# A hybrid diffusion step on one core: triangular blocks turned by VectorE, condition vectors on four column groups, six stores moved

## Chip, core and metric

One core of one Trainium2 chip. The time is device microseconds of one execution of the whole program; lower is better. Times are the median of the runs shown.

## What is computed

One layer of a backbone on 128 prompt tokens and 2048 latent tokens of width 1024, then a final RMSNorm. A layer is:

```python
mod = silu(cond) @ ada_w + ada_b            # shift, scale, gate: 3 x 1024
h = rmsnorm(x, norm_g) * (1 + scale) + shift
p = h @ w_in                                # 1024 -> 2832 columns
y_a = gated DeltaNet, two directions, 4 heads of 64, chunks of 64 tokens
y_b = spatial gating MLP; y_c = pooling minus identity; y_d = 2-D DFT, real part
out = concat(y_a, y_b, y_c, y_d) @ w_out
x + gate * out
```

DeltaNet needs, for each chunk, head and direction, the inverse of a 64x64 unit triangular matrix (`Tinv` in the reference), and a scan over chunks that carries a 64x64 state. Everything is float32; the kernel also returns the prompt's last scan states.

## The kernel before

The kernel is written in a tile framework: each operation is bound to an engine by hand, and a planner at build time puts the operations in an order for each engine by priority (program order, moved by offsets), by when their inputs are ready in its model, and by free buffers. So an edit can change the order of operations that it does not name. All transfers are issued from the queue of SP, in order.

The tokens are 17 tiles of 128, in three groups (12, 12 and 10 chunks of 64).

**Prologue.** `ada_load` brings a quarter of the shift and scale weights, 4 tiles of 512 KB, and `mod_q` (L377) multiplies them by the two condition vectors: of each quarter two tiles as float32 (L386; a float32 matmul is two passes, two instructions in the trace) and two split into a rounded part and a rest by ScalarE or VectorE (L391 to L394) and multiplied as float32r (L397). The result lies as 4 rows of 512 columns; L403 turns it into columns. Meanwhile `x_prep` loads x tiles, adds the position table and scales by the norm; `x_fin` (L334) transposes them on TensorE (L342), ScalarE applies scale and shift (L344), VectorE and GpSimd split the result into `hT`. The list `late` holds six x tiles; L467 stores them to `xs_d`, from which the output phase reads them again.

**Projections.** `mm3` (L250) is three float32r products for one float32 product; its matmuls are most of TensorE's work. `proj_cm` calls `tick` after each piece, and `tick` advances the generators in the list `work`: `lanes` of a group, later `gate_rows`. One step is taken if one generator is in the list, two if there are more.

**The triangular inverse.** `pair_pre` (L647) builds, for a pair of heads, products of keys in PSUM (L673, L703) with decays; the two 32x32 diagonal blocks of each 64x64 matrix go to `Ld`, the block between them to `Lo`. A lane is one diagonal block; `lanes_in` (L727) puts a lane on a partition with 32 transposes on TensorE (L731) for each group and 16 ScalarE copies (L734). `lanes_solve` (L736) runs 30 steps of two VectorE operations each (L741, L743) on all lanes. `lanes_out` (L750) goes back: 128 small products with the identity for each group (L767, two instructions each), after 4 strided VectorE copies (L762), then copies with masks on ScalarE (L771), on VectorE (L772) and to `XE` on ScalarE (L775). Two chains of 32x32 products (L783 to L793) fill in the block between. `rec_out` stores the results for the scan.

**After phase A.** `gate_rows` (L1283) multiplies the last third of `ada_w` by the condition vectors, float32 with two columns of weights (L1295), out of two of the four buffers of the pool `xp_`; the remaining branches, the scan (L1033 on), the Fourier branch and the output projection (`out_tile`) follow.

PSUM has tags of `pj` 3, `pa` 2, `pb` 2 and `pc` 1 banks. `x_fin` in phase A uses `pc` alone, key products use `pb`, the lanes use `pa`.

Of the kernel before, what the change touches and what calls it, by code (L numbers as in the profile page):

```python
# [9 lines left out]
F32 = mybir.dt.float32  # L10
# [7 lines left out]
D = 1024  # L18
# [126 lines left out]
def tile_dit_step(ctx: ExitStack, tc: tile.TileContext, io: dict, dbg=None, stop=None):  # L145
# [112 lines left out]
    c4 = cst.tile([128, KC, 4], F32R, name="c4")  # L258
    nc.scalar.activation(c4[:, :, 0:2], csil, AF.Copy)
    nc.vector.tensor_tensor(c4[:, :, 2:4], csil, c4[:, :, 0:2].bitcast(F32), op=ALU.subtract)  # L260
    s42 = cst.tile([4, 2], F32, name="s42")
    nc.vector.tensor_tensor(s42, ident[0:4, 0:2], ident[0:4, 2:4], op=ALU.add)
# [71 lines left out]
    def x_fin(prep, fs=range(KC), pss=(pc,)):  # L334
        with hp(OXv[0]):
# [3 lines left out]
            for f in fs:  # L339
# [7 lines left out]
                if spill is not None:  # L347
                    nc.sync.dma_start(out=h_d[spill, :, f, off:off + 384], in_=h[:, :384])

# [12 lines left out]
    with tc.tile_pool(name="ada", bufs=3, reuse_waits="tile") as ada_p:  # L362
        OXv[:] = [0, 0]
        c40 = ada_p.tile([128, KC, 4], F32, name="c40", bufs=1)
        nc.vector.memset(c40, 0.0)
        nc.vector.tensor_copy(c40[:, :, 0:2], csil)
# [10 lines left out]
        def mod_q(q, ts):  # L377
            ps = pb()
            for s in range(2):
                for k0 in range(0, KC, 4):  # L380
                    t = ts[2 * s + k0 // 4]
                    sp = ("0", "0", "1", "2")[2 * s + k0 // 4]
                    o = ps[0:4, s * 256:s * 256 + 256]
                    if sp == "0":
                        for k in range(4):
                            nc.tensor.matmul(o, c40[:, k0 + k], t[:, k], start=(k0 + k == 0), stop=(k0 + k == KC - 1))  # L386
                        continue
                    hi = ada_p.tile([128, 4, 256], F32R, tag="adh", name="adh", bufs=2)
                    lo = ada_p.tile([128, 4, 256], F32R, tag="adl", name="adl", bufs=2)
                    if sp == "1":  # L390
                        nc.scalar.activation(hi, t, AF.Copy)  # L391
                    else:
                        nc.vector.tensor_copy(hi, t)
                    nc.vector.tensor_tensor(lo, t, hi.bitcast(F32), op=ALU.subtract)  # L394
                    for e, w in enumerate((hi, lo)):
                        for k in range(4):
                            nc.tensor.matmul(o, c4[:, k0 + k], w[:, k],  # L397
                                             start=(k0 + k + e == 0), stop=(k0 + k + e == KC))
# [1047 lines left out]
```

## Time and profile before

| | us |
|---|---|
| median of 3 runs | 1212.36 (1209.45 to 1213.25) |
| the profiled execution, its own time | 1211.1 |
| its span, first to last instruction | 1209.3 |
| TensorE busy / VectorE busy / ScalarE busy | 1090.1 / 815.1 / 417.9 |

The profiled execution stands 1.26 us under the median. Its granted TensorE clock is 0.952 of full on the mean. In the trace PE is TensorE's matmuls, PEld its weight loads, DVE is VectorE, ACT ScalarE, POOL GpSimd, SPq the queue of SP.

### The profile page before, as it was taken

How to read it: one execution, taken by the hardware profiler on the slowest of the kernel's cores; microseconds unless marked ns; L12 is line 12 of the kernel's file. 1: busy time of each engine (PE TensorE's matmuls, PEld its weight loads, DVE VectorE, ACT ScalarE, POOL GpSimd, SP SyncE). 2: the span in 40 equal slices, each digit the busy share in tenths (PEclk: the TensorE clock that was granted, in tenths of full speed). 3: DMA queues.
4: the chain of work that ended last, by engine and by line, in shares of the span. 5: the costliest groups of instructions: out<-in, count | busy, mean ns of one | idle time of the engine just before them, and what ended most of it. 6: DMA issues, size and time to landing. Idle time of an engine off the chain costs nothing.

```text
span 1209.3 us, 29864 instructions
## 1 busy us (share of the span) xinstructions
PE 1090.1 (90%) x12211; PEld 986.3 (82%) x12211; DVE 815.1 (67%) x1864; ACT 417.9 (35%) x837; POOL 432.6 (36%) x429
## 2 busy tenths in 40 slices
PE   5888988998799698898979989898999889999997
PEld 2488977998779697875879888887899778999997
DVE  3666886799974699934884633784243488878665
ACT  2355667656565756123123111121111211111211
POOL 1347364726442237510231242232135343433212
PEclk9899998999879799898999999999999989999999
DMA  9879549943644564645264556589355645544331
GB/s 309 302 250 316 139 120 232 279 131 83 148 114 104 126 151 112 192 142 143 70 187 125 160 165 211 181 262 306 89 160 167 213 136 166 173 133 150 106 131 70
DMA packets 251391, 204.28 MB, mean 169 GB/s; under 512 B 109138, under 2 KB 218706, under 8 KB 250998
## 3 DMA queue, kind: packets, MB, share of 16 engines
q1 hardware_dynamic: 251254, 202.37, 56.7%
q8 instruction: 96, 1.57, 0.5%
q14 instruction: 41, 0.34, 0.1%
HBM read 138.86 MB, written 63.46 MB: 167 GB/s over the span
## 4 chain that ended last, share of the span: by engine, by line
PE 45%; DVE 17%; DMA 11%; issue 4%; ACT 3%; SPq 1%; POOL 1%; DVEq 0%; ACTq 0%; POOLq 0%
PE pj L250 34%; PE pa L1053 3%; DMA wst<-in_wt_dram 2%; DVE LL L743 2%; DVE ltmp L741 2%; DVE BIG L243 2%; DVE acc L842 1%; DMA X<-xd_d 1%; DMA ada<-in_ada_dram 1%; PE pb L1295 1%; DMA hr<-h_d 1%; DMA wos<-in_wo_dram 1%; DVE BIG L240 1%; DMA wst<-in_wv_dram 1%; PE pb L1393 1%
## 5 line engine op out<-in xcount | busy, mean ns | idle before, releaser
L250 PE MATMUL pj<-BIG 128*128 128x256 f32 (+4 forms) x3888 | 615.9, 313 | 16.7 <-ACT g L1222 4.0
L250 PEld LDWEIGHTS pj<-BIG 128*128 128x128 f32 x3888 | 560.9, 195 | 36.2 <-issue 10.8
L250 PE MATMUL pj<-BIG,yh 128*128 128x256 f32 x1088 | 197.5, 286 | 3.6 <-ACT BIG L1355 2.4
L243 POOL TENSOR_TENSOR BIG<-wst,BIG 128x512 fp32r<-128x512 f32 (+1 forms) x66 | 96.0, 1455 | 235.4 <-DVE BIG L240 137.3
L250 PEld LDWEIGHTS pj<-BIG,yh 128*128 128x128 f32 x1088 | 164.6, 190 | 7.0 <-ACT BIG L1355 2.6
L250 PE MATMUL pj<-BIG,yl 128*128 128x256 f32 x544 | 141.3, 284 | 0.0
L250 PEld LDWEIGHTS pj<-BIG,yl 128*128 128x128 f32 x544 | 98.7, 190 | 0.7
L240 DVE CAST BIG<-wst 128x512 fp32r<-128x512 f32 (+2 forms) x72 | 38.6, 540 | 74.8 <-DMA wst<-in_wt_dram 34.5
L1060 POOL TENSOR_TENSOR gS<-S,sc_s 128x256 f32<-128x256 f32 x32 | 20.9, 655 | 133.8 <-DVE S L1075 128.3
L842 DVE SCALAR_TENSOR_TENSOR acc<-raw,prm,acc 128x768 f32<-128x768 f32 (+1 forms) x72 | 64.2, 908 | 5.5 <-ACT acc L840 5.5
L1374 ACT ACTIVATE yh<-yt 128x768 fp32r<-128x768 f32 (+1 forms) x34 | 20.7, 629 | 128.9 <-issue 47.3
L1222 ACT ACTIVATE g<-pj 128x256 f32<-128x256 f32 (+1 forms) x64 | 23.3, 396 | 118.3 <-PE pj L250 111.8
L243 DVE TENSOR_TENSOR BIG<-wst,BIG 128x512 fp32r<-128x512 f32 (+1 forms) x66 | 53.4, 808 | 15.9 <-ACT BIG L242 13.8
L1413 POOL TENSOR_TENSOR z<-z,xs 128x1024 f32<-128x1024 f32 x16 | 41.8, 2612 | 57.1 <-DVE z L1405 52.0
L741 DVE TENSOR_TENSOR ltmp<-LL 128x60 f32<-128x60 f32 (+14 forms) x90 | 53.6, 595 | 4.5 <-ACT LL L734 3.1
L743 DVE TENSOR_TENSOR LL<-LL,ltmp 128x60 f32<-128x60 f32 (+14 forms) x90 | 55.3, 614 | 1.4
L242 ACT ACTIVATE BIG<-wst 128x512 fp32r<-128x512 f32 (+1 forms) x60 | 37.6, 632 | 35.3 <-DMA wst<-in_wt_dram 14.0
L354 POOL TENSOR_TENSOR BIG<-h,BIG 128x384 fp32r<-128x384 f32 (+2 forms) x28 | 26.7, 953 | 54.0 <-DVE BIG L353 37.4
L1075 DVE TENSOR_TENSOR S<-pa,gS 128x256 f32<-128x256 f32 x34 | 14.3, 420 | 42.1 <-PE pc L1053 35.0
L1375 DVE TENSOR_TENSOR yl<-yt,yh 128x768 fp32r<-128x768 f32 (+1 forms) x34 | 37.3, 1112 | 7.8 <-ACT yh L1374 7.8
L1405 DVE TENSOR_TENSOR z<-pj,gbc 128x256 f32<-128x256 f32 x68 | 26.0, 419 | 22.5 <-PE pj L250 22.2
L1071 ACT ACTIVATE xn<-pa 128x256 f32<-128x256 f32 x34 | 12.9, 381 | 80.8 <-PE pa L1053 73.2
(291 smaller groups left out, 1846.1 us busy)
## 6 DMA issues: line engine op xcount, KB each, us to landing
wst<-in_wt_dram SPq DMA_DIRECT2D x96, 256.0 KB, 3.5
R<-rec_d SPq DMA_DIRECT2D x136, 128.0 KB, 3.1
ada<-in_ada_dram SPq DMA_DIRECT2D x24, 512.0 KB, 5.3
C<-com_d SPq DMA_DIRECT2D x68, 128.0 KB, 3.1
xs<-xs_d SPq DMA_DIRECT2D x16, 512.0 KB
out_dram<-z SPq DMA_DIRECT2D x16, 512.0 KB, 3.1
x<-in_xs_dram SPq DMA_DIRECT2D x13, 512.0 KB
xs_d<-x SPq DMA_DIRECT2D x13, 512.0 KB, 6.1
```

The source lines that it names most:

```text
L240: nc.vector.tensor_copy(hi[:, ks, a:a + w], st[:, :, :w])
L242: nc.scalar.activation(hi[:, ks, a:a + w], st[:, :, :w], AF.Copy)
L243: (nc.vector if k0 == 0 else nc.gpsimd).tensor_tensor(lo[:, ks, a:a + w], st[:, :, :w], hi[:, ks, a:a + w].bitcast(F32), op=ALU.subtract)
L250: nc.tensor.matmul(out, lh[a](k), rh[b](k), start=(k == first and i == 0), stop=(k == last and i == 2))
L354: (nc.gpsimd if f % 2 else nc.vector).tensor_tensor(hT[1][:, f, off:off + w], h, hi.bitcast(F32), op=ALU.subtract)
L741: nc.vector.tensor_tensor(tv, X[:, :, j, j + 1:32].unsqueeze(2).to_broadcast([128, 2, j, ni]), bc(X[:, :, 0:j, j], ni), op=ALU.mult)
L743: nc.vector.tensor_tensor(X[:, :, 0:j, j + 1:32], X[:, :, 0:j, j + 1:32], tv, op=ALU.add)
L842: nc.vector.scalar_tensor_tensor(o, raw[:, si + j:si + j + n], w[:, j:j + 1], o, op0=ALU.mult, op1=ALU.add)
L1053: nc.tensor.matmul(ps[o, q], lh(q)[hp], rh[hp, q])
L1375: nc.vector.tensor_tensor(yl[:, q], yt[:, q], yh[:, q].bitcast(F32), op=ALU.subtract)
L1405: nc.vector.tensor_tensor(z[:, ns], ps, gbc[:, cd, ns], op=ALU.mult)
L1413: nc.gpsimd.tensor_tensor(z, z, xs, op=ALU.add)
```

## The change

It has five parts. (1) The lanes are formed and undone by VectorE transposes of 32x32 blocks: two in `lanes_in` and four in `lanes_out` for each group, each over 1024 elements of 128 partitions; the sign moves into the factor `nb`; ScalarE copies diagonal blocks into `XA`, whose other halves GpSimd clears; `LL` has one buffer. (2) The products of keys take PSUM from `pa`, and `x_fin` in phase A alternates between `pc` and `pa`. (3) `mod_q` and `gate_rows` multiply by 32 columns of weights (two of them not zero) at one of four column positions, all in float32 and without a split; a product with `gsum` adds the four parts. (4) A store of 6x8 elements from `h67` to `xs_d` stands ahead of the six stores of `late`, which write over it and so come after it. (5) Steps of the generators: `lanes` has 20 where it had 30, `gate_rows` 10 where it had 16.

```diff
-    c4 = cst.tile([128, KC, 4], F32R, name="c4")
...
+    c32 = cst.tile([128, KC, 32], F32, name="c32")
+    nc.gpsimd.memset(c32, 0.0)
+    nc.vector.tensor_copy(c32[:, :, 0:2], csil)
+
+    def strip_mm(ps, k, w):
+        g = 32 * (k % 4)
+        nc.tensor.matmul(ps[g:g + 32], c32[:, k], w, start=k < 4, stop=k >= 4, tile_position=(0, g))
+
+    gsum = cst.tile([128, 2], F32, name="gsum")
+    nc.vector.tensor_tensor(gsum, ident[:, 0:2], ident[:, 32:34], op=ALU.add)
+    for j in (64, 96):
+        nc.vector.tensor_tensor(gsum, gsum, ident[:, j:j + 2], op=ALU.add)
@@ mod_q @@
-                for k0 in range(0, KC, 4):
-                    t = ts[2 * s + k0 // 4]
-                    sp = ("0", "0", "1", "2")[2 * s + k0 // 4]
...
-                    nc.vector.tensor_tensor(lo, t, hi.bitcast(F32), op=ALU.subtract)
-                    for e, w in enumerate((hi, lo)):
-                        for k in range(4):
-                            nc.tensor.matmul(o, c4[:, k0 + k], w[:, k],
-                                             start=(k0 + k + e == 0), stop=(k0 + k + e == KC))
-            rows = ada_p.tile([4, 512], F32, tag="mrow", name="mrow", bufs=1)
-            nc.scalar.activation(rows, ps[0:4, :], AF.Copy)
+                for k in range(KC):
+                    strip_mm(ps[:, s * 256:s * 256 + 256], k, ts[2 * s + k // 4][:, k % 4])
+            rows = ada_p.tile([128, 512], F32, tag="mrow", name="mrow", bufs=1)
+            nc.scalar.activation(rows, ps, AF.Copy)
             ps = pb()
             for j in range(4):
-                nc.tensor.matmul(ps[:, 2 * j:2 * j + 2], rows[:, j * 128:(j + 1) * 128], s42)
+                nc.tensor.matmul(ps[:, 2 * j:2 * j + 2], rows[:, j * 128:(j + 1) * 128], gsum)
@@ prologue @@
-        x_fin(p1, (6, 7), (pa,))
+        h67 = x_fin(p1, (6, 7), (pa,))
         xd_k(range(3), 3)
         x_fin(p2, range(8), (pc, pa))
         fold_pool()
+        nc.sync.dma_start(out=xs_d[0:len(late), 0, 0:8], in_=h67[0:len(late), 0:8])
         for i, xt in late:
             nc.sync.dma_start(out=xs_d[i], in_=xt)
@@ scalars @@
+        nc.vector.tensor_scalar(g.nb, g.be, -1.0, None, op0=ALU.mult)
@@ pair_pre (both products: keys by keys, keys by queries) @@
-            ps = pb()
+            ps = pa()
...
-            nc.gpsimd.tensor_tensor(Ldv[:, pair, d], Ldv[:, pair, d], bc(g.be[:, pair, d], 32), op=ALU.mult)
+            nc.gpsimd.tensor_tensor(Ldv[:, d], Ldv[:, d], bc(g.nb[:, pair, d], 32), op=ALU.mult)
@@ lanes @@
-    def lanes_in(Ld, LL, jbs=range(8)):
-        for jb in jbs:
-            ps = pa()
-            for j in range(4):
-                nc.tensor.transpose(ps[:64, j * 128:j * 128 + 128], Ld[:, :, jb * 4 + j], ident)
-            pv = ps[:64].rearrange("p (j c b i) -> p j c b i", c=2, b=2, i=32)
-            for c2, cp in enumerate(HALF):
-                nc.scalar.activation(LL[cp, jb * 4:jb * 4 + 4], pv[:, :, c2], AF.Copy, scale=-1.0)
+    def lanes_in(Ld, LL, d):
+        nc.vector.transpose(LL[:, d], Ld[:, d].rearrange("p l j -> p j l"))
...
+    def lanes_tile(g):
+        t = ln_.tile([128, 3072], F32, tag="L6", name="XF", bufs=1)
+        XA = t.rearrange("p (r x) -> p r x", r=2)[:, :, :2 * g.nch * 64].rearrange("p r (d c j) -> p r d c j", d=2, j=64)
+        for d in range(2):
+            nc.gpsimd.memset(XA[:, :, d, :, 32 * d:32 * d + 32], 0.0)
+        return XA
...
-        for d in (1, 0):
-            for b8 in range(4):
...
-                for e in range(8):
-                    for c2, cp in enumerate(HALF):
-                        rows = slice(c2 * 64, c2 * 64 + nu)
-                        nc.tensor.matmul(ps[cp, e * nu:e * nu + nu], X2[rows, e], ident[rows, rows])
...
+        XD, XE = [None, None], [None, None]
+        for d, flip in ((1, 0), (0, 0), (0, 1), (1, 1)):
+            t = LL[:, d] if flip else ln_.tile([128, 32, 32], F32, tag=f"XT{d}", name="XT", bufs=1)
+            te = t.rearrange("p l e -> p e l")
+            nc.vector.transpose(te, te if flip else LL[:, d])
+            t = t[:, :2 * nch].rearrange("p (r c) e -> p r c e", r=2)
+            if flip == d:
+                XE[d] = t
+            else:
+                XD[d] = t
                 for c2 in range(2):
-                    q = slice(c2 * 64 + 32 * (1 - d), c2 * 64 + 32 * (1 - d) + 32)
-                    nc.scalar.activation(XE[q, :, :, sl], pv[q, 1 - d], AF.Copy)
-                yield 1
+                    for b in range(2):
+                        q = slice(c2 * 64 + b * 32, c2 * 64 + b * 32 + 32)
+                        nc.scalar.activation(XA[q, :, d, :, b * 32:b * 32 + 32], t[q], AF.Copy)
+            yield 1
...
@@ phase_a @@
-            x_fin(preps.pop(0))
+            x_fin(preps.pop(0), range(KC), (pc, pa))
...
-                    LL = ln_.tile([128, 32, 2, 32], F32, tag="LL", name="LL", bufs=2)
                     def lanes():
-                        for jb in range(8):
-                            lanes_in(Ld, LL, (jb,))
+                        LL = ln_.tile([128, 2, 32, 32], F32, tag="LL", name="LL", bufs=1)
+                        for d in range(2):
+                            lanes_in(Ld, LL, d)
                             yield 1
                         lin.pop()
+                        XA = lanes_tile(g)
@@ gate_rows @@
                 for k in range(4):
-                    nc.tensor.matmul(o, csil[:, 4 * kh + k], sb[:, k], start=(kh == 0 and k == 0), stop=(kh == 1 and k == 3))
-                    if k % 2:
-                        yield 1
+                    strip_mm(ps[:, q % 2 * 256:q % 2 * 256 + 256], 4 * kh + k, sb[:, k])
+                yield 1
             if q % 2:
                 n = slice(q // 2 * 512, q // 2 * 512 + 512)
+                rows = xp_.tile([128, D], F32, tag="x", name="grow")[:, :512]
+                nc.scalar.activation(rows, ps, AF.Copy)
+                ps = pb()
+                nc.tensor.matmul(ps[0:2], gsum, rows)
                 nc.vector.tensor_tensor(gt[0:2, n], ps[0:2], bt[0:2, n], op=ALU.add)
+                yield 1
```

## Rows read from the trace of the kernel before

**Rows 1.** Page of the profile, busy time, share and instructions of each engine.

```profile
PE 1090.1 (90%) x12211; PEld 986.3 (82%) x12211; DVE 815.1 (67%) x1864; ACT 417.9 (35%) x837; POOL 432.6 (36%) x429
```

**Rows 2.** Busy us of PE, PEld, DVE, ACT, POOL by stretch; clock, DMA, GB/s.

```profile
0.00:60.00 60.00, 40.17 (x205) 21.62 (x206) 30.24 (x60) 17.43 (x28) 13.36 (x15) 0.91 0.92 308
210.00:240.00 30.00, 29.46 (x319) 28.47 (x318) 21.39 (x43) 20.09 (x39) 24.27 (x21) 1.00 0.96 285
240.00:330.00 90.00, 78.90 (x597) 74.49 (x597) 89.32 (x161) 48.79 (x85) 41.28 (x41) 0.94 0.47 117
330.00:390.00 60.00, 57.97 (x638) 49.85 (x637) 37.02 (x103) 35.22 (x80) 20.53 (x29) 0.86 0.45 108
390.00:450.00 60.00, 49.70 (x778) 45.95 (x777) 45.77 (x106) 39.78 (x83) 20.04 (x26) 0.89 0.59 138
450.00:510.00 60.00, 52.18 (x457) 49.79 (x455) 59.33 (x111) 22.41 (x35) 37.47 (x50) 0.96 0.59 157
510.00:540.00 30.00, 28.94 (x447) 24.02 (x448) 9.86 (x22) 9.70 (x27) 2.91 (x4) 0.85 0.46 152
540.00:600.00 60.00, 53.17 (x612) 42.66 (x609) 38.02 (x80) 15.83 (x41) 6.13 (x4) 0.94 0.40 108
600.00:660.00 60.00, 53.42 (x886) 49.56 (x886) 43.42 (x82) 17.57 (x52) 15.38 (x14) 0.97 0.49 144
```

**Rows 3.** The same by stretch, instructions of line 731 alone (TensorE, its weight loads).

```profile
210.00:240.00 30.00, 2.61 (x18) 2.15 (x19) 1.00 0.96 285
240.00:330.00 90.00, 3.79 (x14) 1.86 (x14) 0.94 0.47 117
390.00:450.00 60.00, 5.36 (x32) 3.53 (x32) 0.89 0.59 138
540.00:600.00 60.00, 4.78 (x32) 3.47 (x32) 0.94 0.40 108
```

**Rows 4.** The same by stretch, instructions of line 767 alone.

```profile
330.00:390.00 60.00, 15.70 (x256) 13.25 (x256) 0.86 0.45 108
510.00:540.00 30.00, 9.86 (x256) 9.36 (x256) 0.85 0.46 152
600.00:660.00 60.00, 8.64 (x256) 7.93 (x256) 0.97 0.49 144
```

**Rows 5.** Groups of instructions: shapes, count, busy us, mean ns, idle before, releasers.

```profile
L767 PE MATMUL pa<-cm,LL 48*64 48x48 f32 (+1 forms) x384 | 18.4, 253 | 6.1 <-DVE LL L743 4.0 <-ACT XE L775 2.1
L342 PE MATMUL pc<-cm,x 128*128 128x128 f32 (+1 forms) x76 | 17.6, 292 | 9.5 <-DVE x L331 6.3 <-ACT h L344 3.1
```

**Rows 6.** One line's or a timeline's rows: VectorE operations of 512 and 1024 elements.

```profile
L762 DVE COPY X<-LL x12: 590/616/1942, 332.5 to 637.0; 128x512 f32<-128x512 f32 x12
...
503.01 0.42 DVE L240 CAST BIG<-wst 128x512 fp32r<-128x512 f32 x1
...
10.83 1.21 DVE L394 TENSOR_TENSOR adl<-ada,adh 128x1024 fp32r<-128x1024 f32 x1
```

**Rows 7.** Timeline of TensorE: one, two and four groups of columns at work.

```profile
21.44 3.62 PE L386 MATMUL pb<-ada,c 128*4 128x256 f32 x16
...
490.09 1.21 PE L703 MATMUL pb<-sl 64*64 64x64 f32 x40
...
216.98 1.44 PE L673 MATMUL pb<-sl 64*32 64x64 f32 x96
```

**Rows 8.** Busy time by stretch, instructions of line 1295 alone.

```profile
510.00:540.00 30.00, 6.04 (x26) 1.96 (x27) 0.85 0.46 152
540.00:600.00 60.00, 11.24 (x40) 2.82 (x37) 0.94 0.40 108
```

**Rows 9.** Timeline of the queue of SP and of ScalarE, the start.

```profile
44.60 0.35 SPq L467 DMA_DIRECT2D xs_d<-x  x1
...
57.08 5.23 SPq L467 DMA_DIRECT2D xs_d<-x  x3
...
64.94 1.20 ACT L344 ACTIVATE h<-pa,modab 128x384 f32<-128x384 f32 x2
```

More of the change, by code (lines that the diff above doesn't have):

```diff
@@ L348, in x_fin @@
                     nc.sync.dma_start(out=h_d[spill, :, f, off:off + 384], in_=h[:, :384])
+            return h
     def h_split(h, f, off):
@@ L363, in tile_dit_step @@
         OXv[:] = [0, 0]
-        c40 = ada_p.tile([128, KC, 4], F32, name="c40", bufs=1)
-        nc.vector.memset(c40, 0.0)
-        nc.vector.tensor_copy(c40[:, :, 0:2], csil)
         def ada_load(q):
@@ L526, in make_group @@
         g.ns = 12 if gi < 2 else 8
-        for nm, sh in (("P", [128, 2, 2, 12]), ("be", [128, 2, 2, 12]), ("eA", [128, 2, 2, 12]), ("eB", [128, 2, 2, 12]),
+        for nm, sh in (("P", [128, 2, 2, 12]), ("be", [128, 2, 2, 12]), ("nb", [128, 2, 2, 12]), ("eA", [128, 2, 2, 12]), ("eB", [128, 2, 2, 12]),
                        ("Pp", [128, 2, 2, 12]), ("Pn", [128, 2, 12]), ("bmx", [128, 2, 12]), ("m1s", [128, 2, 12]),
@@ L698, in pair_pre @@
             cs = slice(h2 * nT, h2 * nT + nT)
-            ps = pb()
+            ps = pa()
             for t in range(nT):
@@ new lines, in lanes_solve, with lanes_out @@
+        dg = LL.rearrange("p d c i -> p d (c i)")
+        for d in range(2):
+            nc.gpsimd.memset(dg[:, d, 0:31 * 33 + 1:33], 1.0)
+    def lanes_tile(g):
[4 more added lines that the diff above has]
+        return XA
+    def lanes_out(g, LL, Lo, XA):
+        nch = g.nch
+        XF = [XA[:, r] for r in range(2)]
+        XD, XE = [None, None], [None, None]
[8 more added lines that the diff above has]
+                XD[d] = t
@@ L915, in phase_a @@
         if gi:
-            x_fin(preps.pop(0))
+            x_fin(preps.pop(0), range(KC), (pc, pa))
         if gi == 1:
-            x_fin(preps.pop(0))
+            x_fin(preps.pop(0), range(KC), (pc, pa))
         elif gi == 2:
-            x_fin(preps.pop(0))
-            x_fin(x_prep([(16, 128)], 512, None))
+            x_fin(preps.pop(0), range(KC), (pc, pa))
+            x_fin(x_prep([(16, 128)], 512, None), range(KC), (pc, pa))
         lg = sm_.tile([128, 6, 16], F32, tag="lg", name="lg", bufs=1)
@@ L961, in post @@
                         tick()
-                    blk[:] = [ln_.tile([128, 64, 32], F32, tag="Ld", name="Ld", bufs=1),
+                    blk[:] = [ln_.tile([128, 2, 32, 32], F32, tag="Ld", name="Ld", bufs=1),
                               ln_.tile([128, 2, NCC, 32], F32, tag="Lo", name="Lo", bufs=3)]
-                    nc.gpsimd.memset(blk[0][:, g.nu:], 0.0)
+                    nc.gpsimd.memset(blk[0][:, :, 2 * g.nch:], 0.0)
                 Ld, Lo = blk
@@ L967, in post @@
                 if pair == 1:
-                    LL = ln_.tile([128, 32, 2, 32], F32, tag="LL", name="LL", bufs=2)
                     def lanes():
-                        for jb in range(8):
-                            lanes_in(Ld, LL, (jb,))
+                        LL = ln_.tile([128, 2, 32, 32], F32, tag="LL", name="LL", bufs=1)
+                        for d in range(2):
+                            lanes_in(Ld, LL, d)
                             yield 1
                         lin.pop()
+                        XA = lanes_tile(g)
                         for a, b in zip(SPL, SPL[1:]):
@@ L977, in lanes @@
                             yield 1
-                        yield from lanes_out(g, LL, Lo)
+                        yield from lanes_out(g, LL, Lo, XA)
                     lin.append(1)
```

49 lines of the change are left out of this document (7 added, 42 removed).

## The prediction

> **What bounds the kernel now.** I read the page first: TensorE is busy 90% of the span and VectorE 67% [rows 1], so an edit that takes work off TensorE is worth something only where TensorE is what holds the end. Then I cut phase A into stretches and looked at both engines in each [rows 2]. Three kinds are to be seen. In the first 60 us TensorE is busy for 40.2 us and the transfers are the bound (DMA share 0.92, 308 GB/s). From 240 to 330 and from 450 to 510 us VectorE is busy 89.3 of 90 and 59.3 of 60 us: there TensorE's work is cover, not the bound. In 210 to 240, 330 to 390 and 510 to 540 us TensorE is busy for 96 to 98% of the stretch, and VectorE has time to spare: there a microsecond off TensorE is a microsecond off the kernel. Between them lie 390 to 450 and 540 to 660 us, where TensorE is busy 83 to 89% and neither engine holds the time by itself. I take the full gain in the TensorE stretches, none in the VectorE stretches and half in the others. That weighting is my choice; its ends are the first two rivals.
>
> The clock speaks the same way: 330 to 390 us, where the products of line 767 stand thickest, has a granted clock of 0.86 on the mean of its time at 1.2 and 2.4 GHz, and 256 of these instructions took 15.7 us there, against 8.6 us in 600 to 660 us at 0.97 [rows 2, 4].
>
> **The change part by part.** *Lanes off TensorE.* The 96 transposes (line 731) go: 2.6 us in 210 to 240 (full), 3.8 us in 240 to 330 (none), 5.4 and 4.8 us in the mixed stretches (half, 2.7 and 2.4) [rows 3]. The 768 products with the identity (line 767) go: 15.7 and 9.9 us in TensorE stretches (full) and 8.6 us in a mixed one (half, 4.3) [rows 4]. Together 2.6 + 2.7 + 2.4 + 15.7 + 9.9 + 4.3 = 37.6 us of the 50.8 us that they occupy. The first half of line 767 also had TensorE idle for 6.1 us, for VectorE's last step and ScalarE's copies [rows 5]; I count half, 3.1 us. The chains of 32x32 products stay.
>
> *Lanes on VectorE.* Eighteen transposes of 1024 elements come, six for each group. The trace has none, so I bound one. A VectorE operation of 1024 elements with two sources took 1.21 us. All six read or write word by word with a step of 32 words; what such a step costs is shown by line 762, whose 512 strided elements took 0.616 us in the median, where 512 adjacent ones took 0.42 [rows 6]. That is 1.47 times, so I take 1.21 x 1.47 = 1.8 us. The lower end is twice the adjacent copy, 0.84 us, the upper twice the longest strided one, 2 x 1.942 = 3.9 us. Eighteen come to 32 us; the 12 strided copies that go give back 12 x 0.62 = 7.4 us, and the masked copies of line 772 go too (not counted). What lies on a path: `lanes_in` of groups 0 and 1 falls in or just ahead of the VectorE stretches, 4 x 1.8 = 7.2 us lost (3.4 to 15.6 us by the ends). The other fourteen fall where VectorE has time. In the queue of VectorE the taps of the convolution and the splits of weights stand behind each transpose and are late by its length; TensorE waits for them if its own pieces run out.
>
> The Trainium skill (Vector Engine (DVE) Microarchitecture Reference, Measured stream behaviour on trn2) speaks against this part: a stream whose words do not come in adjacent pairs moves at 1.7 to 2.5 ns a column in place of 1.05. By it a transpose would take 1.8 to 2.6 us, and the sum would end up to 3 us later. The strided row above agrees in kind.
>
> *ScalarE and GpSimd.* 120 copies go from ScalarE and 24 longer ones come; GpSimd clears six halves of a tile and VectorE makes three small negations. ScalarE is 35% and GpSimd 36% busy [rows 1], and the chains of products now read VectorE's tile, not ScalarE's copies, so I cost these at nothing; if the clears came late, the copies behind them would hold only the store of the result.
>
> *Condition vectors.* A float32 pass of 256 columns with four columns of weights took 3.62 us / 16 = 226 ns, so 57 ns for 64 columns. Products of 64 columns that share their 64 rows of the array and write two groups of columns took 1.21 us / 40 = 30 ns each, those that write four took 1.44 us / 96 = 15 ns [rows 7]. So time goes down with the number of column groups, and I take 4 x 15 = 60 ns for a pass of a strip. `gate_rows` has 64 passes, 3.8 us, and two products with `gsum` of 512 columns, four passes of 2 x 226 ns, 1.8 us: 5.6 us against 17.3 us, two thirds off. Of 6.0 us in 510 to 540 that is 4.0 (full), of 11.2 us in 540 to 600 it is 7.5, half of it 3.7 [rows 8]: 7.7 us. Its steps also start earlier, since `lanes` has fewer of them; I count nothing for that, because its loads still go through two free buffers.
>
> The Trainium skill (TensorE: Matmul & The Clock Gate, The mechanism) has a rule against the strips: a weight load runs beside matmuls in flight only if its row group differs, and all four strips use all rows. By it the strips would go one after another, which is the third rival. The rows of products that share their rows do not bear it out.
>
> *The start.* In each quarter 32 strip passes, 1.9 us, stand for 3.6 us of float32 passes and as many float32r ones, and the split on ScalarE and VectorE goes; with the split gone I estimate 3 us on the way from the last weights to the last shift and scale. Three of the six stores were on the queue by 44.60 us, ahead of the data of the second x tiles, and the other three from 57.08 us on; the ScalarE operation that makes the last pieces of `hT` ran only at 64.94 us, behind the squares of those x tiles [rows 9]. Three stores of 0.52 MB (128 x 1024 float32) at 308 GB/s are 5.1 us of the transfers. Together 8 us; the ends are 0 (the x data are late anyway) and 13 (all six stores count, 10 us, and 3). What is put off is not free: the tiny store waits for the last `h` in the queue of SP, and the six stores, 10 us of transfers, then stand before the first projection's weights and the next x tiles. TensorE's remaining prologue covers that; without the cover three more stores than now would be ahead, 5 us.
>
> *PSUM.* TensorE waited 3.1 us on ScalarE in `x_fin` with one bank [rows 5]; with three I take half, 1.5 us (0 to 3). Key products now share `pa` with the lanes, which need it less; the projections between them hide that.
>
> **The sum.** 37.6 + 3.1 - 7.2 + 7.7 + 8 + 1.5 = 50.7 us. From the profiled execution's 1211.1 us that is 1160.4 us; the median of the runs is 1.3 us above that execution, which I leave out. After phase A nothing is removed, so the rest should move forward as it is.
>
> **The rivals.**
> 1. *All of it lands.* The planner fills TensorE everywhere and the low clock goes with the small products: 50.8 + 6.1 + 11.4 + 13 + 3.1 - 3.4 = 81 us, 1130 us. For it: TensorE is the busiest engine throughout. Against: VectorE's two full stretches.
> 2. *VectorE becomes the bound from 210 to 510 us.* It is busy there for 252.8 of 300 us [rows 2], and the transposes add to it. Then the gains up to 450 us are lost, 2.6 + 15.7 + 2.7 = 21 us: 1181 us. For it: the full stretches would grow at both ends. Against: 23 us of VectorE's time are free in 330 to 390 us.
> 3. *The strips run in turn.* A pass and its load, 226 ns and about 75 ns (2.82 us / 37) [rows 7, 8], make 19.3 us of 64 passes in `gate_rows` and 1.8 us more: the 7.7 us are lost and 2.5 us added; the start has 128 passes, 38 us, so its 8 us are lost and I estimate 9 us added. 1187 us.
> 4. *Slower: the transposes are dear.* From 210 to 660 us VectorE is busy for 344.1 of 450 us [rows 2]. With 18 transposes of X us and 7.4 us gone it fills these 450 us at X = 6.3 us, and with the start's 8 us the kernel is slower from X = 6.7 us; at 9 us it would end 41 us later, 1252 us. For it: no row shows a transpose. Against: the worst strided copy of 512 elements took 1.942 us.
> 5. *Nothing to be seen.* The planner's new order gives back as idle what is saved; or the stores are not put off in effect, which alone would be 1168 us, inside the forecast.
>
> **How the numbers follow.** Forecast (1145 to 1176 us) 0.56, rival 1 0.15, rival 2 0.17, rival 3 0.05, rival 4 0.04, rival 5 (no change) 0.03. A difference of 0.3%, some 3.6 us, is what a measurement can tell here. The first four cases are faster, 0.93; same 0.03; slower 0.04. The range takes the forecast, the near two thirds of rival 1 and most of rival 2: 1130 to 1186 us.
>
> **What would show it.** Right: no instructions of lines 731 and 767, TensorE's busy time near 1015 us, 18 VectorE transposes near 1.8 us, strip passes some 60 ns apart, the first projections about 8 us earlier, and 330 to 390 us shorter with a higher clock. Wrong: transposes over 4 us, strip passes over 200 ns apart, VectorE full from 210 to 510 us, or TensorE idle by more than now (119 us of the span) for loads behind the six stores.

## The result and the profile after

The changed kernel takes 1196.8 us (median of 4 runs, 1196.1 to 1198.8), the kernel before beside it 1212.3 us: a ratio of 0.9875 (95% interval 0.9844 to 0.9907). That is faster by 15.5 us, where 50.7 us were forecast, and 1196.8 us lies outside the stated range of 1130 to 1186 us. The sign was right and the size was not.

The page's busy line after [rows 1], and the mean granted clock (kernel before: 1209.3 us, clock 0.952):

```profile
PE 1046.3 (87%) x11351; PEld 954.6 (80%) x11351; DVE 818.9 (68%) x1837; ACT 386.2 (32%) x734; POOL 433.2 (36%) x436
...
core 0: 1197.0 us, clock 0.919
```

TensorE was to be busy for some 1015 us and is busy for 1046.3. The stretches of phase A after, same columns as [rows 2]:

```profile
0.00:60.00 60.00, 32.70 (x215) 19.23 (x216) 21.56 (x55) 16.87 (x31) 15.70 (x18) 0.69 0.87 274
...
210.00:240.00 30.00, 25.49 (x240) 24.54 (x240) 18.76 (x34) 12.82 (x27) 19.00 (x19) 0.89 0.86 251
240.00:330.00 90.00, 76.51 (x558) 70.79 (x557) 88.64 (x166) 48.67 (x79) 38.48 (x40) 0.93 0.51 129
330.00:390.00 60.00, 45.45 (x461) 40.33 (x460) 46.75 (x107) 35.34 (x66) 27.41 (x30) 0.79 0.48 119
390.00:450.00 60.00, 50.82 (x709) 48.49 (x709) 50.92 (x108) 35.85 (x71) 22.15 (x30) 0.89 0.61 141
450.00:510.00 60.00, 55.66 (x384) 54.30 (x383) 58.16 (x103) 16.01 (x31) 34.11 (x48) 0.97 0.54 153
510.00:540.00 30.00, 21.46 (x573) 16.10 (x574) 15.67 (x28) 10.90 (x17) 4.60 (x5) 0.81 0.61 167
540.00:600.00 60.00, 51.87 (x312) 40.72 (x313) 53.69 (x99) 10.28 (x25) 7.97 (x10) 0.81 0.39 111
600.00:660.00 60.00, 52.12 (x777) 47.28 (x776) 36.65 (x75) 15.12 (x37) 17.18 (x13) 0.97 0.78 219
```

Two things are to be seen. Where TensorE had been busy for 96 to 98% of the time (210 to 240, 330 to 390, 510 to 540) it now pauses for 15 to 28% of it, so the work that went left pauses behind. And in 330 to 390 the clock is 0.79, where it was 0.86: the low clock did not go with the small products. VectorE is busy for 369.2 us from 210 to 660 (the sum of the eight rows), where it was busy for 344.1.

**The clock of the opening.** The profile's record of the granted clock begins at the first change of level, 17.0 us into the span before and 13.3 us after, and the page counts full speed until then. The durations say that it was the low level. A strip pass (L264) that lies within a recorded stretch of 2.4 GHz takes 379 to 403 ns; those ahead of the first record take 631 to 634 ns in the kernel after (before, passes of 256 columns take 589 to 634 ns ahead of it and 274 to 380 ns at 2.4 GHz). In four runs below (strips_only, tensore_work_back, held_back_cut, held_after_filled_more) the record begins only at 50 to 56 us, behind all 128 strip passes of the start, and these took 604 to 637 ns each. In strips_only the page gives them a clock of 1.00, though they were busy for longer than after, at 0.69 (16.61 and 15.91 us for the same 128 passes, line 264 alone):

```profile
0.00:60.00 60.00, 16.61 (x128) 3.84 (x128) 1.00 1.00 318
```

So I count the opening as 1.2 GHz. The first 60 us, where transfers are the bound, then have a clock of 0.58 after, where it was 0.77 (the rows say 0.69 and 0.91), and the whole spans 0.913 and 0.945 (the pages say 0.919 and 0.952). From 60 us on the record is complete in all runs.

**Who got the lead?** Three kinds of rows, with the start of the first and the last instruction: ScalarE's copies of projections for the convolution, VectorE's last step of each turn of the scan, and the output tiles. First the kernel before, then after:

```profile
L823 ACT ACTIVATE raw<-pj x42: 270/474/547, 117.4 to 445.6; 128x384 f32<-128x384 f32 x12, 128x392 f32<-128x392 f32 x12, 128x320 f32<-128x320 f32 x6, 128x192 f32<-128x192 f32 x6
...
L1075 DVE TENSOR_TENSOR S<-pa,gS x34: 410/419/426, 680.8 to 1088.7; 128x256 f32<-128x256 f32 x34
...
L1405 DVE TENSOR_TENSOR z<-pj,gbc x68: 410/418/427, 980.6 to 1201.2; 128x256 f32<-128x256 f32 x68
```

```profile
L805 ACT ACTIVATE raw<-pj x42: 268/472/502, 120.1 to 450.0; 128x384 f32<-128x384 f32 x12, 128x392 f32<-128x392 f32 x12, 128x320 f32<-128x320 f32 x6, 128x192 f32<-128x192 f32 x6
...
L1057 DVE TENSOR_TENSOR S<-pa,gS x34: 409/424/426, 649.2 to 1056.4; 128x256 f32<-128x256 f32 x34
...
L1390 DVE TENSOR_TENSOR z<-pj,gbc x68: 409/423/427, 974.1 to 1188.8; 128x256 f32<-128x256 f32 x68
```

The lanes gained: the scan begins 31.6 us earlier and ends 32.3 us earlier. The projections gained nothing: the last of their copies here is 4.4 us later. So more projections are left when the scan starts, 1610 passes in place of 1470 (first before from 666 us on, then after from 634 us on), and the end, which needs both, is 12.4 us earlier:

```profile
L250 PE MATMUL pj<-BIG 128*128 128x256 f32 x1470 | 200.8, 291 | 3.5 <-ACT u L1222 2.3 <-ACT g L1222 1.2
```

```profile
L250 PE MATMUL pj<-BIG 128*128 128x256 f32 x1610 | 220.2, 292 | 0.0
```

**Where the time is, on TensorE's account.** I laid TensorE's busy times over the stretches of its granted clock, with the opening as 1.2 GHz. "Work" counts busy time at 2.4 GHz whole and at 1.2 GHz half; "low" is the other half; "pauses" is the rest of the span. The three sum to the span (us). "Low" is the most that the low clock can add: eight strip passes took 1.08 us at 1.2 GHz and 0.64 at 2.4, 1.7 times and not twice. The forecast's row is the span before less 50.7 us and busy time of 1015 us, with "low" as before, since it gave the clock no term:

```
run                       span    work    low  pauses
before                  1209.3  1037.9   52.2   119.2
forecast                1158.6   962.8   52.2   143.6
after                   1197.0   968.9   77.4   150.7
lanes_only              1200.6   993.1   65.2   142.3
strips_only             1238.7  1015.4   91.2   132.0
stores_only             1234.6  1036.2   67.0   131.3
tensore_work_back       1240.1   998.2   93.4   148.5
held_back_cut           1258.4  1002.1  120.3   135.9
held_before_products    1208.1  1027.9   58.0   122.2
held_before_solve       1195.0  1038.6   43.4   113.0
held_after_solve        1181.3   968.9   68.4   144.0
held_after_filled       1190.6  1002.7   65.1   122.8
held_after_filled_more  1185.1  1023.4   46.0   115.7
```

The work fell by 69.0 us, near the forecast's 75.1, and pauses grew by 31.5 us, where the forecast's figures imply 24.4. Of the 38.4 us that the span is over the forecast, 25.2 stand under "low". This is bookkeeping of one execution each, not yet a cause: the experiments ask what the end waits for.

### The profile page after: what moved, and what is told of

It is laid out like the page before. It is cut to its first block, busy times and chain, and to the rows that moved or that the text cites. A ratio compares the mean times of both kernels' runs of the same rounds, so it can differ in the third digit from the quotient of the medians.

```text
span 1197.0 us, 27975 instructions
## 1 busy us (share of the span) xinstructions
PE 1046.3 (87%) x11351; PEld 954.6 (80%) x11351; DVE 818.9 (68%) x1837; ACT 386.2 (32%) x734; POOL 433.2 (36%) x436
## 4 chain that ended last, share of the span: by engine, by line
PE 41%; DVE 27%; DMA 17%; issue 6%; ACT 4%; SPq 2%; POOL 2%; DVEq 0%; ACTq 0%; POOLq 0%
PE pj L250 32%; DMA wst<-in_wt_dram 4%; PE pa L1035 3%; DMA ada<-in_ada_dram 3%; DVE LL L727 3%; DVE acc L824 3%; DVE ltmp L725 3%; DMA pr<-in_cpr_dram 2%; DVE BIG L243 2%; DVE BIG L361 1%; DVE acc L871 1%; SPq L1024 1%; DVE BIG L240 1%; DVE BIG L362 1%; DVE LL L748 1%
## 5 line engine op out<-in xcount | busy, mean ns | idle before, releaser
L250 PE MATMUL pj<-BIG 128*128 128x256 f32 (+4 forms) x3888 | 630.8, 319 | 25.6 <-ACT raw L805 5.6
L250 PEld LDWEIGHTS pj<-BIG 128*128 128x128 f32 x3888 | 578.1, 201 | 50.7 <-issue 11.0
L243 POOL TENSOR_TENSOR BIG<-wst,BIG 128x512 fp32r<-128x512 f32 (+1 forms) x66 | 93.3, 1414 | 215.2 <-DVE BIG L240 131.2
L240 DVE CAST BIG<-wst 128x512 fp32r<-128x512 f32 (+2 forms) x72 | 35.0, 487 | 75.7 <-DMA wst<-in_wt_dram 35.4
L824 DVE SCALAR_TENSOR_TENSOR acc<-raw,prm,acc 128x768 f32<-128x768 f32 (+2 forms) x72 | 66.3, 942 | 1.6 <-ACT acc L822 1.6
L243 DVE TENSOR_TENSOR BIG<-wst,BIG 128x512 fp32r<-128x512 f32 (+1 forms) x66 | 49.8, 754 | 24.3 <-ACT BIG L242 20.7
L242 ACT ACTIVATE BIG<-wst 128x512 fp32r<-128x512 f32 (+1 forms) x60 | 37.7, 633 | 38.4 <-DMA wst<-in_wt_dram 17.9
L264 PE MATMUL pb<-ada,c 128*32 128x256 f32 x192 | 22.1, 566 | 31.7 <-DMA ada<-in_ada_dram 21.4
L1057 DVE TENSOR_TENSOR S<-pa,gS 128x256 f32<-128x256 f32 x34 | 14.3, 421 | 50.6 <-PE pc L1035 45.3
L362 POOL TENSOR_TENSOR BIG<-h,BIG 128x384 fp32r<-128x384 f32 (+2 forms) x28 | 29.1, 1041 | 44.5 <-DVE BIG L361 38.7
L1360 DVE TENSOR_TENSOR yl<-yt,yh 128x768 fp32r<-128x768 f32 (+1 forms) x34 | 40.4, 1206 | 4.1 <-ACT yh L1359 3.9
```

The costliest lines, as they stand in the source:

```text
L240: nc.vector.tensor_copy(hi[:, ks, a:a + w], st[:, :, :w])
L242: nc.scalar.activation(hi[:, ks, a:a + w], st[:, :, :w], AF.Copy)
L243: (nc.vector if k0 == 0 else nc.gpsimd).tensor_tensor(lo[:, ks, a:a + w], st[:, :, :w], hi[:, ks, a:a + w].bitcast(F32), op=ALU.subtract)
L250: nc.tensor.matmul(out, lh[a](k), rh[b](k), start=(k == first and i == 0), stop=(k == last and i == 2))
L362: (nc.gpsimd if f % 2 else nc.vector).tensor_tensor(hT[1][:, f, off:off + w], h, hi.bitcast(F32), op=ALU.subtract)
L824: nc.vector.scalar_tensor_tensor(o, raw[:, si + j:si + j + n], w[:, j:j + 1], o, op0=ALU.mult, op1=ALU.add)
```

## The experiments

Theories: **V**, VectorE holds phase A, and TensorE's freed time becomes pauses; **C**, the low clock behind the pauses costs time by itself; **P**, the planner's new order ate the gain; against them the prediction's own, TensorE holds the end.

**The parts alone.** The first three kernels take the diff's lanes with their PSUM tags; `strip_mm` with `gsum`, `mod_q` and `gate_rows`; and the small store alone. The fourth is the changed kernel with TensorE's work put back:

```diff
+            ps = pa()
+            for j in range(4):
+                nc.tensor.transpose(ps[:64, j * 128:j * 128 + 128], Ld.rearrange("p d l j -> p (d l) j")[:, :, jb * 4 + j], ident)
...
+                        nc.tensor.matmul(ps[cp, e * g.nu:e * g.nu + g.nu], t[rows, k:k + 2].rearrange("p a b -> p (a b)"), ident[rows, rows])
```

> The kernel before with the lanes part alone (VectorE transposes for TensorE's transposes and products with the identity, and the PSUM tags that go with it); float32 condition vectors and stores as before. The prediction's terms for it are 37.6 + 3.1 - 7.2 = 33.5 us, so 1179 us. Theory V (VectorE holds phase A, where 210 to 360 us was full after the change, and the time freed on TensorE becomes pauses): 1198 to 1208 us. Theory P (the planner's new order ate a gain that each part has by itself): below 1185 us.

> The kernel before with the condition vectors on four groups of columns alone (start and gate_rows). The prediction's terms are 7.7 us for gate_rows and 3 us at the start: 1201.6 us. Theory V: the start is given back in the first group of phase A, and gate_rows lies where VectorE has time, so 4 to 8 us are left: 1204 to 1208 us. Theory P: near 1201 us or less.

> The kernel before with the six x stores held back by the small store alone. The prediction's term is 5.1 us: 1207 us. Theory V: nothing, 1209 to 1215 us, since the six stores then stand before the loads of the first group. Theory P: 1207 us or less.

> The changed kernel with the 96 TensorE transposes and as many small products with the identity as before put back beside the VectorE transposes, into PSUM that nothing reads; all else as after the change. If TensorE holds phase A, as the prediction had it, these cost what the prediction gave for taking them away, 34 to 38 us: 1231 to 1235 us. Theory V: they run in TensorE's pauses and keep its clock up, 0 to 10 us: 1197 to 1207 us. If the pauses cost by the clock alone, it could even be faster, by up to 5 us.

Measured: lanes 1202.4 us, ratio 0.9899 (0.9855 to 0.9942); strips 1239.5 us, 1.0195 (1.0146 to 1.0243); stores 1233.8 us, 1.0148 (1.0081 to 1.0214); work back 1235.8 us, 1.0170 (1.0106 to 1.0234). The lanes are near V. Two parts that take work away or only move it are slower alone by 24 and 18 us, which no theory had, and 50.1 us of work put back cost 39 us, as the prediction's theory would have it. So at least one thing more is at work. The trace of strips_only names one. Before, then strips_only:

```profile
340.00:380.00 40.00, 39.91 (x495) 33.61 (x495) 24.22 (x61) 18.48 (x46) 15.95 (x18) 0.79 0.47 106
380.00:420.00 40.00, 29.70 (x536) 28.00 (x535) 23.21 (x58) 28.05 (x55) 9.59 (x16) 0.87 0.49 120
```

```profile
340.00:380.00 40.00, 32.50 (x315) 26.85 (x316) 21.77 (x58) 11.45 (x23) 12.77 (x17) 0.62 0.32 80
380.00:420.00 40.00, 40.00 (x243) 29.69 (x242) 12.72 (x35) 20.35 (x44) 5.58 (x11) 0.67 0.23 61
```

The edit does not touch what runs there, but the planner ordered it anew, and the clock is 0.62 and 0.67: from 380 to 420 us TensorE is busy for all of 40 us, most of it at 1.2 GHz. What it did before the clock fell (at 393.6 us, until 427.7) stands in the timeline of strips_only: projection passes of 320 columns, eight in a row in 1.35 us, and then single ones in turn with two small products of the lanes (L754), a turn each 0.59 us, later 0.94 us:

```profile
376.05 1.35 PE L250 MATMUL pj<-BIG 128*128 128x320 f32 x8
...
390.90 0.31 PE L754 MATMUL pa<-cm,X 48*64 48x48 f32 x2
391.14 0.41 PE L250 MATMUL pj<-BIG 128*128 128x320 f32 x1
...
398.20 0.45 PE L754 MATMUL pa<-cm,X 48*64 48x48 f32 x2
398.58 0.63 PE L250 MATMUL pj<-BIG 128*128 128x320 f32 x1
```

So the page's "busy" covers passes that came one at a time. In the table "low" is 39.0 us more than in the kernel before, 8.8 of them in the first 60 us; the run lost 25.4 us. That the low clock cost it the time was not tried.

The trace of stores_only shows what goes with the other loss. Before, stores_only, after:

```profile
60.00:90.00 30.00, 26.86 (x200) 24.50 (x199) 20.13 (x52) 17.03 (x35) 13.53 (x15) 1.00 0.72 247
```

```profile
60.00:90.00 30.00, 26.84 (x178) 24.39 (x178) 15.65 (x41) 13.27 (x28) 8.68 (x11) 0.89 0.88 308
```

```profile
60.00:90.00 30.00, 26.48 (x189) 24.79 (x188) 14.70 (x41) 13.65 (x27) 10.86 (x12) 0.94 0.95 328
```

The stores that were put off now stand where the next loads want to be. With them the prologue's last products (`fold_pool`) come 7.1 us earlier than before in stores_only and 6.8 us after, but the first copy of group 0 comes at 123.2 and 120.1 us, where it was 117.4: the lead is more than given back within 50 us.

**The order kept.** Here the planner runs as in the kernel named, and the instructions are cut afterwards, each in its place.

```diff
+    def half(a):
+        return copy.replace(a, ap=tuple((2 * s, n) for s, n in a.ap), dtype=mybir.dt.bfloat16, offset=2 * a.offset + 1)
...
+            if j % 3 == 0:
+                CUT.update((m1.ins.name, m2.ins.name))
...
+        return copy.replace(a, ap=tuple(a.ap[:1]) + tuple((s, 1) for s, n in a.ap[1:]))
...
+        return copy.replace(a, ap=tuple(a.ap[:1]) + ((1, 1),))
```

`half` is for both operands of the products of lines 731 and 767; `m1` and `m2` are the two operations of a step of the solve, cut to one word; the last line cuts what tensore_work_back had put back to one column.

> The kernel before with every engine's order kept: after the planner is done, the lanes' 96 TensorE transposes and 384 products with the identity read the upper halves of their words as bfloat16, so that each is one short pass in place of float32 passes; the values are rounded, nothing else changes. They occupied 50.8 us of TensorE and I estimate that a third is left. If TensorE holds the stretches as the prediction weighted them (37.6 + 3.1 of 50.8 us), two thirds of that come off: 27 us, 1185 us. Theory V (VectorE holds phase A): 5 to 10 us, 1203 to 1208 us. Theory P (the time was lost to the new order): as the prediction, 1185 us, since the order is kept.

> The kernel before with every engine's order kept, and every third step of the triangular solve cut to one word for each partition (the solve's result is not the full one): some 36 us less of VectorE between 230 and 620 us. By the prediction's weighting VectorE holds 150 of these 390 us, so 10 to 15 us: 1198 to 1203 us. Theory V: 20 us or more, 1193 us or less. Theory P says nothing here.

> The changed kernel with every engine's order kept and the same third of the solve cut: some 36 us less of VectorE, as much as the eighteen transposes brought. Theory V: 25 us or more, 1172 us or less, since VectorE is full from 210 to 360 us and from 420 to 480 us. Theory P: no more than in the kernel before, 10 to 15 us, 1182 to 1187 us.

> The kernel of the run with TensorE's work put back, with that kernel's order kept, and the products and transposes that were put back cut to one column each after planning. If it was their time on TensorE that cost 39 us there, most of it comes back: 1200 to 1208 us. Theory P (it was the order that the planner made around them): 1222 to 1234 us. Theory V agrees with P here.

Measured: held_before_products 1211.8 us, 0.9976 (0.9941 to 1.0010); held_before_solve 1198.7 us, 0.9864 (0.9824 to 0.9903); held_after_solve 1185.3 us, 0.9762 (0.9714 to 0.9811); held_back_cut 1260.0 us, 1.0375 (1.0319 to 1.0431). What the cuts took away is smaller than I had written. The products of line 767 in held_before_products:

```profile
L767 PE MATMUL pa<-cm,LL 48*64 48x48 bf16 (+1 forms) x192 | 6.7, 203 | 6.9 <-DVE LL L743 4.1 <-ACT XE L775 2.8
L767 PE MATMUL pa<-cm,X 48*64 48x48 bf16 (+1 forms) x192 | 6.0, 195 | 3.0 <-ACT XE L775 3.0
```

They fell from 34.2 us to 12.7; the transposes did not (18.0 us, where they had taken 16.6). Some 20 us of TensorE gave 1.6 us, at most 7 by the interval. The prediction would have had 16 (its 40.7 of 50.8 us). Not all 20 us were work: in the table 10.0 us of work went, "low" grew by 5.8 us and pauses by 3.0. The solve with its cut, in the kernel before and then in the changed one:

```profile
L743 DVE TENSOR_TENSOR LL<-LL,ltmp 128x1 f32<-128x1 f32 (+10 forms) x90 | 48.9, 543 | 1.4
L741 DVE TENSOR_TENSOR ltmp<-LL 128x1 f32<-128x1 f32 (+10 forms) x90 | 44.5, 495 | 4.9 <-ACT LL L734 3.4
```

```profile
L727 DVE TENSOR_TENSOR LL<-LL,ltmp 128x1 f32<-128x1 f32 (+10 forms) x90 | 46.9, 521 | 1.5
L725 DVE TENSOR_TENSOR ltmp<-LL 128x1 f32<-128x1 f32 (+10 forms) x90 | 42.2, 468 | 1.6
```

The solve took 108.9 us uncut before and 110.8 after, so 15.5 us less of VectorE gave 14.8 us in the kernel before, and 21.7 us less gave some 11.5 us (15.7 by the profiled spans) in the changed one. The two times lie in the ranges that were given for the prediction's weighting and for P, but those were worked out for 36 us. For 15.5 us the weighting (150 of 390 us) gives 6 us, and 14.8 came, so this speaks for V: with the order kept, a microsecond of the solve is worth 0.5 to 1, one of the small products 0.1. By the table over half of what the solve gave back is low clock that did not come (8.8 of 14.3 us and 9.0 of 15.7 us of the spans). It says so of the solve, which is one chain; not of all that VectorE does.

held_back_cut failed as a cut: a product of one column took about as long as one of 48 (37.0 against 35.0 us in all), and the transposes, products now, two instructions each, went from 15.1 to 24.3 us. But it came out 24 us slower than its twin of the same order, with 4 us more of work by the table, and the mean clock is lower, first tensore_work_back, then held_back_cut:

```profile
core 0: 1240.1 us, clock 0.926
```

```profile
core 0: 1258.4 us, clock 0.907
```

(With the opening 0.905 and 0.885.) "Low" went from 93.4 to 120.3 us. That speaks for C, but the products' busy time grew with it, by 11 us, so it does not show it.

**The order alone.** Two or four clears of 784 words on VectorE that nothing needs.

```diff
+        if gi == 0:
+            inert = cv_.tile([128, 784], F32, tag="raw", name="inert")
+            nc.vector.memset(inert, 0.0)
+            nc.vector.memset(inert, 0.0)
```

> The kernel before with two clears of 784 words, which nothing needs, on VectorE at the head of the first group: some 1 us of work, but the planner then makes another order (2,534 moves of TensorE's 9,080 instructions are not counted here; over a tenth stand elsewhere). Theory P (the order of the kernel before is a lucky one, which any edit loses, and that is where the expected gain went): 10 to 25 us slower, 1222 to 1238 us, like the two parts that were slower alone. Theory V with the clock (pauses on VectorE's account and the low clock behind them, whatever the order): within 6 us, 1207 to 1220 us.

> The same with four clears, some 2 us of work: a third order of the kernel before. Theory P: 10 to 25 us slower, 1222 to 1238 us. Theory V with the clock: 1207 to 1221 us.

> The changed kernel with the same two clears: another order of the same work. Theory P: its own order is a draw like any other, so this is as likely faster as slower, within 15 us, 1182 to 1212 us. Theory V with the clock: 1194 to 1202 us.

> The changed kernel with the two clears at the head of the second group: a third order. Theory P: 1182 to 1212 us, and not near the run before it. Theory V with the clock: 1194 to 1202 us.

(The number in brackets in the first belongs to another pair of orders; nothing rests on it.) Measured: the kernel before 1224.1 and 1222.4 us, 1.0091 (1.0055 to 1.0127) and 1.0077 (1.0042 to 1.0112); the changed one 1203.6 and 1207.4 us, 0.9909 (0.9877 to 0.9940) and 0.9945 (0.9920 to 0.9971). All four lie within the ranges given for P and above those for V with the clock, though the last two came out near each other, which P had not. A new order of the same work cost both kernels something, 11 to 12 us and 7 to 11 us in the medians, so both seem to have a good one. It makes up half of what strips and stores lost alone, but not the missing gain: the mean of the two new orders differs by 17.8 us between the kernels, much as their own orders do. So P is right that an order can be lucky, falls as the explanation of the missing gain, and stays as a scatter of some 10 us in every comparison across orders.

**The clock.** Into the finished order of the changed kernel go products of 112 float32 columns that nobody reads, into the longer pauses of its trace. In the first run some of them add to columns that are in use, so part of the values changes; in the second they have columns of their own.

```diff
+                reps, back = FILL[k]      # k: TensorE's k-th matmul, reps: about 0.7 or 0.85 of the pause
...
+                    out.append(copy.replace(eye, name="I-%d" % (9000000 + 100 * k + m), outs=(to,), ins=(copy.replace(w, ap=(w.ap[0], (1, 112))), w),
```

> The changed kernel with every engine's order kept, and some 130 products of 112 float32 columns that nothing reads, put into TensorE's longer pauses (over 1 us in the trace of after, from 49 us on; about 70% of each is filled). Theory C (the low clock costs time by itself): the clock falls less often, the 26 us that the low clock takes beyond the kernel before shrink by half, 1180 to 1189 us. If the low clock only goes along with the pauses: 1195 to 1205 us, since what is waited for comes no sooner and the fillers can be in the way. If TensorE's work as such holds the end: 1210 us and more.

> The changed kernel with every engine's order kept and 209 products of 112 float32 columns in TensorE's pauses of over 0.6 us (85% of each by the trace of after), all into columns that nothing else uses, so the computation is the changed kernel's. Theory C (the low clock costs time by itself): at least as fast as the first filling, 1182 to 1193 us, with less time at the low clock. If the first filling's gain was from something else: 1195 to 1205 us. If the fillers get in the way: over 1205 us.

Measured: 1192.3 us, 0.9835 (0.9789 to 0.9881), and 1190.3 us (1186.9 to 1194.3), 0.9834 (0.9800 to 0.9869). The second kernel, its clock and two groups:

```profile
core 0: 1185.1 us, clock 0.969
...
L250 PE MATMUL pj<-BIG 128*128 128x256 f32 (+4 forms) x3888 | 610.4, 312 | 20.2 <-ACT g L1204 4.3 <-DVE lg L912 3.7 <-ACT raw L805 2.8
L349 PE MATMUL pj<-cm 128*128 128x112 f32 x256 | 36.7, 291 | 0.0
```

The first time lies between the ranges, the second in that of C. With all fillers TensorE does 59.1 us more (36.7 and 22.4 in two other groups) and the kernel is no slower; its runs all lie below those of after, by 6.5 us in the median, though they were not taken side by side and the intervals of the ratios overlap. The page's 0.969 leaves out the opening, 50.0 us here; from 60 us on the clock is 0.967, where it was 0.931 after. The projections' 3888 passes, untouched, took 630.8 us in after and take 610.4. So the fillers did raise the clock, and C is likely, with a size: 31.4 us of "low" went, and 11.9 us came off the profiled span (the slowest of the four executions of after against the fastest of these six). The rest is back as time in which TensorE is paused or at fillers (pauses fell by 35.0 us, work grew by 54.5). And where work stands decides what it costs: 59.1 us in the pauses were free, 50.1 us in the lanes' own place cost 39 us in tensore_work_back; how much of the 39 is that run's new order, and how much the 16.0 us that its "low" grew, was not separated. This version is the fastest of the study that computes all.

**Less on VectorE, and the stores.** 

```diff
-        nc.vector.tensor_copy(hi, h)
+        nc.scalar.activation(hi, h, AF.Copy)
...
-            nc.vector.tensor_tensor(Pf[:, d], Pf[:, d], bcm(K(("mkf", "mkb")[d]), nch), op=ALU.add)
+            nc.gpsimd.tensor_tensor(Pf[:, d], Pf[:, d], bcm(K(("mkf", "mkb")[d]), nch), op=ALU.add)
...
-        nc.sync.dma_start(out=xs_d[0:len(late), 0, 0:8], in_=h67[0:len(late), 0:8])
```

> The changed kernel with the rounding copy of h (56 operations, some 27 us) on ScalarE in place of VectorE; the planner makes a new order. Theory V (VectorE is what the pauses wait for): 1178 to 1192 us, of which up to 10 us either way is the new order. If VectorE does not matter: 1197 to 1210 us, as the two other orders of the same work.

> The same, and the 12 mask additions of Pf (1 us each) on GpSimd in place of VectorE. Theory V: 1172 to 1190 us. If VectorE does not matter: 1197 to 1210 us, or slower where GpSimd's longer additions stand in the chain.

> The kernel with the lanes part alone and the rounding copy of h on ScalarE. Theory V: 1182 to 1198 us against 1202 us. If VectorE does not matter: 1200 to 1213 us.

> The changed kernel without the small store that holds the six x stores back; the planner makes a new order. If the stores put off are a loss also here (the transfers are full from 60 to 120 us): 1185 to 1198 us, some 5 us and more below the other two orders of the changed kernel (1204 and 1207 us). If they are a gain, as the prediction had it (5 us): 1202 to 1212 us.

Measured: 1198.6 us, 0.9892 (0.9834 to 0.9950); 1226.9 us, 1.0107 (1.0050 to 1.0165); 1203.1 us, 0.9914 (0.9878 to 0.9950); 1194.5 us, 0.9858 (0.9811 to 0.9904). Moving 27 us of VectorE's copies to ScalarE did nothing that can be told from the scatter of orders, so V missed its ranges here; with the mask additions on GpSimd the kernel lost 28 us more, a new order included. So V holds for the solve's chain and was not shown for VectorE's load as a whole. Without the stores put off the changed kernel is as fast as with them, in the range given for a loss; nothing speaks for the 5.1 us, but the scatter of orders is larger than that.

## Why the prediction was wrong

- **Products off TensorE (37.6 + 3.1 us): the step that failed.** It took the stretches in which TensorE is busy 96 to 98% as stretches that TensorE holds, and paid each microsecond in full. With the order kept, 20 us of these products were worth 1.6 us, at most 7, where the prediction's price is 16. The nearly full engine was not the chain that ended these stretches: in the kernel before, the solve on VectorE paid almost one for one (14.8 of 15.5 us) through the same time. Part of the price was lost to the clock: "low" grew by 5.8 us in that run. The lanes alone, transposes included, gave 12 us in place of 33.5.
- **What is left runs at the same clock: assumed without a term.** The prediction even had the clock rise in 330 to 390 us. "Low" grew by 25.2 us, in 29 recorded stretches of 1.2 GHz where there had been 20; taking 31.4 us of it away by fillers gave 6.5 us in the median and 11.9 on the profiled spans. How much of the missing 35 us it is stays open. The Trainium skill (TensorE: Matmul & The Clock Gate, What's actually happening) calls the ramp less than 1% of a typical span. The trace agrees for the ramp at the start, up to the first record of 2.4 GHz (2.3 us of "low" before, 0.2% of the span); the stretches of 1.2 GHz that come later are another matter, and with them "low" is 4.3% of the span before and 6.5% after.
- **Eighteen transposes of 1.8 us: right, their price too low.** They took 35.2 us:

```profile
L748 DVE STREAM_TRANSPOSE LL<-LL 128x1024 f32<-128x1024 f32 x6 | 12.1, 2039 | 0.0
L718 DVE STREAM_TRANSPOSE LL<-Ld 128x1024 f32<-128x1024 f32 x6 | 11.9, 1990 | 0.5 <-POOL Ld L674 0.5
L748 DVE STREAM_TRANSPOSE XT<-LL 128x1024 f32<-128x1024 f32 x6 | 11.2, 1937 | 0.2
```

  1.94 to 2.04 us lies in the estimate of 1.8 to 2.6 us that the prediction worked out from the Trainium skill (Vector Engine (DVE) Microarchitecture Reference, Measured stream behaviour). Rival 4 is out. But four of them were counted, 7.2 us. VectorE has 25.1 us more from 210 to 660; at the solve's 0.5 to 1 that would be 13 to 25 us. That the transposes cost what the solve does was not tried.
- **Strips: they run beside each other, but not at 60 ns.** Line 264 by stretch:

```profile
0.00:60.00 60.00, 15.91 (x128) 3.78 (x128) 0.69 0.87 274
510.00:540.00 30.00, 3.00 (x32) 0.67 (x32) 0.81 0.61 167
540.00:600.00 60.00, 3.23 (x32) 0.76 (x32) 0.81 0.39 111
```

  15.91 us / 128 = 124 ns at the start, 6.23 / 64 = 97 ns in `gate_rows`: no sign of the 300 ns of passes in turn, so rival 3 is out. What is over the 60 ns is in good part the clock, since the rows behind the 60 are all from stretches of 2.4 GHz. Eight passes after, first at 2.4 and then at 1.2 GHz, 80 and 135 ns each:

```profile
14.72 0.64 PE L264 MATMUL pb<-ada,c 128*32 128x256 f32 x8
...
22.66 1.08 PE L264 MATMUL pb<-ada,c 128*32 128x256 f32 x8
```

  The four products with `gsum` in `gate_rows` fell into stretches of 1.2 GHz and took 3.7 us, twice the 1.8 us of the sum. So `gate_rows` saves TensorE 7.3 us, where 11.7 us were forecast.
- **The start (8 us):** 6.8 us arrived at the end of the prologue and none at the first group. The cover that the prediction named was not there: "without the cover three more stores than now would be ahead, 5 us".
- **PSUM (1.5 us):** from 80 us on TensorE's transposes in `x_fin` waited 13.0 us for ScalarE before and 13.1 us after, so the two more banks gave nothing there; the prediction's 3.1 us is one of several groups.
- **"The rest should move forward as it is": wrong.** The scan moved by 32 us and the end by 12, since the projections that phase A had left stand between them.
- Rival 2 (1181 us) had the mechanism nearest to what was seen, VectorE holding 210 to 510 us, and was 16 us too fast.

## What to carry to other kernels

Before an engine's work is removed, hold the planner's order and cut that work to nothing: what the end gives back is its price, and a busy share of 97% did not foretell it. Account for TensorE in three parts, work at full speed, what the low clock adds, and pauses; work that is taken out where something else sets the pace came back in the other two here. And where a planner orders the instructions anew, a part tried alone carries some 10 us of order with it here: compare several orders, or keep one.

## What was not expected of the hardware

TensorE stayed at 1.2 GHz for most of 40 us in which the page shows no idle time (strips_only, 380 to 420 us), with single projection passes and pairs of small products by turns. Cutting 480 small products and transposes to one column made the kernel 24 us slower at the same order; it also made the transposes 9.2 us longer. And 59 us of products that nobody needs, put into its pauses, raised the granted clock from 60 us on from 0.931 to 0.967 and cost nothing.
